# Small TensorE operations queued and issued one at a time between dense matmuls

## The chip, the cores and the metric

The kernel runs on one core of a Trainium2 chip. A core has a matrix engine (TensorE, PE in the profile; its weight loads are listed as PEld), a vector engine (VectorE, DVE), a scalar engine (ScalarE, ACT), GpSimd (POOL) and a queue engine for transfers (SyncE, SP). Each engine works through its own queue in order and waits for others through semaphores. TensorE writes to PSUM, eight banks that VectorE and ScalarE read. The metric is the device time of one execution in microseconds (us); several runs give a median. One further execution is recorded by the hardware profiler; its numbers are those of the profile.

## What is computed

Two layers act on x, 512 tokens by 2048 channels in float32. Both normalize, project, mix along the tokens, gate, project back, and add to the residual; then each adds a gated projection of a second input.

```python
for i in range(DEPTH):
    xn = rms_norm(h, norm_pre[i])
    if i % 2 == 0:
        proj = xn @ ab_w_in[j]                       # 2048 x 8336
        oa = forgetting_attention(...)               # 16 heads of 64, causal softmax
        ob = rwkv7_time_mix(...)                     # 16 heads of 64, a recurrence over tokens
        y = concat([oa * silu(ga), ob * silu(gb)]) @ ab_w_out[j]
    else:
        u, v, g = split(xn @ c_w_in[j])              # 2048 x 6144
        oc = chunked_spatial_gating(u, v, ...)
        y = (oc * silu(g)) @ c_w_out[j]
    h = h + rms_norm(y, norm_post[i])
    h = h + (p[i] @ ple_w_proj[i]) * sigmoid(h @ ple_w_gate[i])
```

## The kernel before

**Dense products.** Every dense operand is split into a high and a low part in a reduced float32 form, and a product is three matmuls: high by high, high by low, low by high. In the first layer `dense_fm` (L205 on) computes 128 output channels for all 512 tokens: it goes through 16 k-tiles of 128 channels, three matmuls each (L213, L214, L215), 512 columns wide. The weights come through `stream`: one transfer into a raw buffer, a cast on ScalarE (`whi`, L197) and a subtraction on VectorE (`wlo`, L199), each buffer holding four k-tiles, four buffers each. From the output product of the first layer on, the large products run in `seven`, which forms seven products of half matrices in place of eight (L1601). Some of these have the weights as the stationary side and 256 moving columns (`fm=True`: the two output products and the first gate), the others 512 moving columns.

**Side work.** While dense products run, everything else is woven in by hand. `weave` takes a list of (beat, step); after each k-tile `beat` counts up and runs the steps that are due. In `seven`, `later` and `tick` do the same. So the order of TensorE's queue is the order written, except where the scheduler of the framework finds that an operation's inputs would not be there in time by its own estimate; it then issues a later one that is ready.

The side steps that the change touches put several small TensorE operations into the queue at once:

- `rwkv_head` (matmuls at L484): for a pair of heads and half of the tokens, four chunks e, and for each the two heads q. The operands of head 0 lie in partitions 0 to 63, those of head 1 in 64 to 127, so each product uses half the rows of the array. The two accumulators are a `tm` tile and the `g` tile. Behind them stand masks on VectorE (L488 on) and copies on ScalarE. There are 16 such calls: eight pairs, two halves. The places are HEAD and HEAD1, in units of a window of 36 beats.
- `rwkv_tokens`: four transposes of the scaled keys (L515) into one `tm` tile, and two of the values (L523) into the next, then copies. 16 calls.
- `rwkv_chain`: the recurrence over eight chunks, three steps a chunk. The third step has the state update (L627) and the two products of the output, L636 and L637, in a row.
- `fox_load`'s `tokens` (L847): four transposes, 8 calls. `fox_probs` (L910): one to four transposes of attention weights, 64 calls, 160 transposes. `fox_values` (L923) multiplies by them.
- `flip` in `last_layer` (L1316): four transposes, 16 calls. `turn` in `layer_c` (L1760): four transposes, 16 calls, of which eight are placed in the second layer's output product.

Products of plain float32 operands (L484, L612 to L637, and the 32x32 ones of `rwkv_inverse` at L551 and L572) are run as two passes of the array; a transpose is one pass. `tm()` gives the names `tm0` and `tm1` in turn; each is one PSUM bank, so a third tile waits for the first. A single transpose of a mixing weight (L1716) and one of 16 rows (L1799) stand alone in `layer_c`; the change leaves them as they are.

Of the kernel before, what the change touches and what calls it, by code (L numbers as in the profile page):

```python
# [16 lines left out]
P = 128  # L17
# [89 lines left out]
class Net:  # L107
# [19 lines left out]
    def tm(self):  # L127
        self.ntm ^= 1
        return f"tm{self.ntm}"
# [76 lines left out]
    def dense_fm(self, wap, c0, xhi, xlo, ps, kts=None):  # L206


        nc = self.nc
        nk = len(xhi)  # L210
        acc = self.t(ps, [P, T], "mm")
        for k, hi, lo in self.stream(wap, c0, P, kts or list(range(nk)), None):
            nc.tensor.matmul(acc, hi, xhi[k], start=(k == 0), stop=False)  # L213
            nc.tensor.matmul(acc, hi, xlo[k], start=False, stop=False)  # L214
            nc.tensor.matmul(acc, lo, xhi[k], start=False, stop=(k == nk - 1))  # L215
            self.beat()
        return acc

    def weave(self, side, late=False):


        rest = [(n - self.beats, step) for n, step in self.side]
        if not late:
            for _, step in rest:
                step()
            rest = []
        self.side, self.beats = sorted([*rest, *side], key=lambda x: x[0]), 0

    def beat(self):
        self.beats += 1  # L230
        while self.side and self.side[0][0] <= self.beats:
# [238 lines left out]
    def rwkv_head(self, st, h, wp, ps):  # L470
# [11 lines left out]
        for e in range(GC):  # L482
# [4 lines left out]
        for n, pp in enumerate(BLOCKS):  # L487
            nc.vector.tensor_tensor(  # L488
                AT[pp], pg[n // 2][pp, :, 0, BLOCKS[n % 2]], self.mB[pp].broadcast_to([32, GC, 32]), ALU.mult
            )  # L490
        nc.vector.tensor_tensor(off, AT, bc(self.lev[1], P, 32), ALU.mult)
        nc.vector.tensor_tensor(off, off, bc(self.idst, P, 32), ALU.add)
        nc.vector.transpose(flip, off)
        for q in range(2):
            nc.scalar.copy(A32[BLOCKS[2 * q]], pg[q][BLOCKS[2 * q], :, 0, 32:64])
# [8 lines left out]
    def rwkv_tokens(self, st, h, wp, ps):  # L504
# [8 lines left out]
        pb = self.t(ps, [P, GC, P], self.tm())  # L513
        for e in range(GC):
            nc.tensor.transpose(pb[:, e, :], BKh[:, e, :], self.ident)  # L515
        BKt = self.t(wp, [P, GC, P], "BKt")
        nc.scalar.copy(BKt, pb)
# [3 lines left out]
        pv = self.t(ps, [P, GC // 2, P], self.tm())  # L521
        for m in range(GC // 2):
            nc.tensor.transpose(pv[:, m, :], v[:, o + m * P : o + m * P + P], self.ident)  # L523
        sv = SV.rearrange("p (m a) q i -> p m a q i", a=2)
        for a, src in enumerate((slice(0, 64), slice(64, 128))):
            nc.scalar.copy(sv[0:64, :, a, 1, :], pv[src, :, 64:128])
            nc.scalar.copy(sv[64:128, :, a, 0, :], pv[src, :, 0:64])
        nc.gpsimd.tensor_copy(UV[0:64, :, 1, :], SV[0:64, :, 1, :])
        nc.gpsimd.tensor_copy(UV[64:128, :, 0, :], SV[64:128, :, 0, :])
        st["hf", h] = dict(SV=SV, UV=UV, BKt=BKt)  # L530
        yield
# [70 lines left out]
    def rwkv_chain(self, st, h, wp, ps):  # L602
# [5 lines left out]
        for e in range(GC):  # L608
# [27 lines left out]
            nc.tensor.matmul(py[:, 0:P], fl(SV), fl(AR[:, e, 2:4, :]), start=True, stop=False)  # L636
            nc.tensor.matmul(py[:, 0:P], uv, st["GR", h][:, e, :], start=False, stop=True)  # L637
            nc.scalar.copy(Yt[0:64, cc * 64 : cc * 64 + 64], py[0:64, 0:64])
            nc.scalar.copy(Yt[64:128, cc * 64 : cc * 64 + 64], py[64:128, 64:128])
            yield  # L640

    def rwkv_fin(self, pr, st, wp, ps):
        nc, c, Yt = self.nc, self.cols, st["Yt"]
        col = lambda n: c[n][:, pr : pr + 1]
        yp = self.parts(Yt, wp, "bs")
# [24 lines left out]
    def rwkv_all(self, dense, first, wp, ps):  # L670
# [62 lines left out]
        def begin(pr):  # L733
            S0 = sts[pr]["hf", 0]["SV"][:, 0]
# [84 lines left out]
    def fox_load(self, pr, cols, dense, wp, ps):  # L819
# [24 lines left out]
        def tokens():  # L844
            pv = self.t(ps, [P, 4, P], self.tm())
            for m in range(4):
                nc.tensor.transpose(pv[:, m, :], vT[:, m * P : (m + 1) * P], self.ident)  # L847
            for q in range(2):
                v4 = V[q].rearrange("p (m t) -> p m t", t=P)
                src = pv[:, :, q * 64 : q * 64 + 64]  # L850
                nc.scalar.copy(v4[:, :, 0:64], src)
# [1251 lines left out]
```

## Time and profile before

| | us |
|---|---|
| median of 3 runs | 2201.89 |
| lowest, highest | 2201.17, 2202.13 |
| the profiled execution | 2202.32 |
| its span, first to last instruction | 2200.6 |
| mean granted TensorE clock | 0.998 |

The first layer's dense products run to about 740 us with the recurrence beside them, and to about 1012 us with the attention; `seven` begins there. The page gives, for each engine, its busy time; matmuls overlap, so the busy time of TensorE counts some stretches twice over in effect, and distances between starts say more than durations. In the timeline, rows of the same line that follow each other at once are merged, with their count behind an x.

### The profile page before, as it was taken

Reading aid. Unit: us, or ns where it says so; the run is one execution under the profiler, and the core shown is the slowest. Engines: PE = TensorE matmul, PEld = TensorE weight load, DVE = VectorE, ACT = ScalarE, POOL = GpSimd, SP = SyncE. Lnnn points to the kernel's source line nnn. Section 1 sums busy time; section 2 is a strip of 40 time slices with the busy share of each in tenths; the row PEclk is TensorE's granted clock in tenths of the full one; section 3 lists DMA queues with packets and bytes.
Section 4 is the critical chain, followed back from the end, with each engine's and each line's share of the span. In section 5 each row is a group of like instructions: output and inputs, shape, how many; then the busy total and the mean of one; then the engine's idle time right before and its main releaser. Section 6 shows DMA issues by size and latency. Waiting matters only on the chain.

```text
span 2200.6 us, 43486 instructions
## 1 busy us (share of the span) xinstructions
PE 2176.7 (99%) x16535; PEld 1870.7 (85%) x16535; DVE 1661.6 (76%) x3227; ACT 1354.0 (62%) x2763; POOL 298.4 (14%) x360
## 2 busy tenths in 40 slices
PE   8999999999999999999999999999999999999998
PEld 7878888888888788889999999887888889999886
DVE  8756677657633687887979978987687688878968
ACT  5545555555543577776767757755576577667754
POOL 2001010101000000000120121111221220120121
PEclk9999999999999999999999999999999999999999
DMA  7322322223233733336688889789779887688696
GB/s 240 94 80 58 90 78 71 71 73 85 69 85 101 214 106 91 106 92 182 151 200 273 215 187 237 177 219 229 171 163 231 184 201 190 146 199 274 191 253 163
DMA packets 304288, 343.35 MB, mean 156 GB/s; under 512 B 15773, under 2 KB 188222, under 8 KB 303054
## 3 DMA queue, kind: packets, MB, share of 16 engines
q1 hardware_dynamic: 237582, 240.93, 35.1%
q0 software_dynamic: 44608, 85.99, 22.7%
q10 hardware_dynamic: 21888, 13.64, 2.2%
q8 instruction: 130, 2.13, 0.4%
q14 instruction: 80, 0.66, 0.1%
HBM read 305.61 MB, written 34.90 MB: 155 GB/s over the span
## 4 chain that ended last, share of the span: by engine, by line
PE 89%; DMA 4%; DVE 3%; ACT 2%; issue 1%; SPq 0%; ACTq 0%; DVEq 0%; POOLq 0%
PE mm L1601 46%; PE mm L213 10%; PE mm L215 9%; PE mm L214 9%; DMA rq<-in_ple_w_gate_dram 2%; PE tm L551 1%; PE tm L572 1%; DMA gz<-gd 1%; PE g L923 1%; DVE wlo L1566 1%; PE pp L340 1%; PE tm L484 1%; PE ch L636 1%; PE tm L910 1%; PE ch L637 1%
## 5 line engine op out<-in xcount | busy, mean ns | idle before, releaser
L1564 ACT CAST whi<-rq 128x512 fp32r<-128x512 f32 x485 | 298.7, 621 | 203.4 <-PE mm L1601 126.1
L213 PE MATMUL mm<-xh,whi 128*128 128x512 f32 x992 | 412.0, 415 | 0.0
L1566 DVE TENSOR_TENSOR wlo<-rq,whi 128x512 fp32r<-128x512 f32 x485 | 331.0, 688 | 99.4 <-ACT whi L1564 96.8
L215 PE MATMUL mm<-xh,wlo 128*128 128x512 f32 x992 | 391.9, 395 | 0.0
L214 PE MATMUL mm<-xl,whi 128*128 128x512 f32 x992 | 390.0, 393 | 0.0
L197 ACT CAST whi<-raw 128x512 fp32r<-128x512 f32 x272 | 167.5, 617 | 148.5 <-PE mm L214 102.5
L199 DVE TENSOR_TENSOR wlo<-raw,whi 128x512 fp32r<-128x512 f32 x272 | 185.7, 695 | 91.7 <-ACT whi L197 68.9
L215 PEld LDWEIGHTS mm<-xh,wlo 128*128 128x128 f32 x992 | 186.4, 188 | 41.1
L213 PEld LDWEIGHTS mm<-xh,whi 128*128 128x128 f32 x992 | 187.1, 189 | 33.4
L214 PEld LDWEIGHTS mm<-xl,whi 128*128 128x128 f32 x992 | 187.3, 189 | 29.8
L1601 PE MATMUL mm<-whi,yh 128*128 128x512 f32 x424 | 137.0, 391 | 0.9 <-ACT whi L1564 0.9
L1601 PE MATMUL mm<-whi,xl 128*128 128x512 f32 x424 | 137.7, 392 | 0.0
L1601 PE MATMUL mm<-whi,yl 128*128 128x512 f32 x420 | 137.6, 393 | 0.0
L1566 DVE TENSOR_TENSOR wlo<-raw,whi 128x512 fp32r<-128x512 f32 x154 | 105.1, 688 | 36.0 <-ACT whi L1564 35.5
L1564 ACT CAST whi<-raw 128x512 fp32r<-128x512 f32 x154 | 94.7, 620 | 60.8 <-PE mm L1601 46.6
L1601 PE MATMUL mm<-xh,whi 128*128 128x256 f32 x696 | 126.9, 283 | 0.0
L1601 PEld LDWEIGHTS mm<-xh,whi 128*128 128x128 f32 x696 | 108.7, 192 | 0.1
L1509 POOL DMA_DIRECT2D rq<-in_c_w_in_dram x56 | 68.5, 1231 | 243.6 <-DVE wlo L1566 164.0
L1566 DVE TENSOR_TENSOR half<-rq,half 128x512 fp32r<-128x512 f32 x111 | 76.3, 688 | 32.6 <-ACT half L1564 32.4
L1601 PE MATMUL mm<-xh,wlo 128*128 128x256 f32 x348 | 98.5, 283 | 0.0
L1564 ACT CAST half<-rq 128x512 fp32r<-128x512 f32 x111 | 68.9, 620 | 47.6 <-PE mm L1601 27.6
L1601 PE MATMUL mm<-xl,whi 128*128 128x256 f32 x520 | 95.5, 284 | 0.1
(534 smaller groups left out, 5156.1 us busy)
## 6 DMA issues: line engine op xcount, KB each, us to landing
raw<-in_ab_w_in_dram SPq DMA_DIRECT2D x128, 512.0 KB, 3.9
rq<-in_c_w_in_dram POOLq DMA_DIRECT2D x56, 512.0 KB, 7.0
rq<-in_c_w_in_dram SPq DMA_DIRECT2D x50, 512.0 KB, 6.1
rq<-in_ple_w_gate_dram SPq DMA_DIRECT2D x44, 512.0 KB, 6.6
rq<-in_ple_w_gate_dram POOLq DMA_DIRECT2D x36, 512.0 KB, 9.1
raw<-in_c_w_in_dram SPq DMA_DIRECT2D x26, 512.0 KB, 7.9
rq<-in_c_w_out_dram SPq DMA_DIRECT2D x24, 512.0 KB, 4.5
rq<-in_ab_w_out_dram POOLq DMA_DIRECT2D x20, 512.0 KB, 6.9
```

Source lines behind the costliest of these rows:

```text
L197: nc.scalar.copy(hi[:, : m * n], src)
L199: self.weng.tensor_tensor(lo[:, : m * n], src, f(hi[:, : m * n]), ALU.subtract)
L213: nc.tensor.matmul(acc, hi, xhi[k], start=(k == 0), stop=False)
L214: nc.tensor.matmul(acc, hi, xlo[k], start=False, stop=False)
L215: nc.tensor.matmul(acc, lo, xhi[k], start=False, stop=(k == nk - 1))
L340: nc.tensor.matmul(acc, mat, part, start=(j == 0), stop=(j == 1))
L484: nc.tensor.matmul(pg[q][:, e], BK[pp, e].rearrange("p a t -> p (a t)"), AR[pp, e, q::2, :], start=True, stop=True)
L551: nc.tensor.matmul(px[dst, e, :], a[src, e, :], b[src, e, :], start=True, stop=True)
L1509: nc.gpsimd.dma_start(view(tl), block(*where), accum_op=ALU.add)
L1564: self.cast = nc.scalar.copy(hi, src)
L1566: nc.vector.tensor_tensor(lo, src, f(hi), ALU.subtract)
L1601: nc.tensor.matmul(o, x, y, start=(first and r == 0 and j == 0 and not a), stop=(r == 7 and j == 2), **more)
```

## The change

A queue `pe` is added. `spread` puts a step's TensorE operations into it, with what has to follow the last of them (`end`). The first goes out at once if the queue is empty. Each further one goes out from `between`, which is called after the first and the second matmul of each k-tile in `dense_fm`, after the third where no side step is due, and after every matmul in `seven`; it is tied behind the matmul before it with `issue_after`, which orders the two on their engine and adds no wait on another. `drain` empties the queue: before a new `tm` tile while operations on PSUM tiles of that kind are pending, at every `weave`, before `rwkv_fin`, the start of a pair, `fox_values`, and the last output product. In the products with 256 moving columns (`packed`) the queue is emptied at once, so that a step's operations stand in a row there as before.

In `rwkv_head` one operation of the queue is both products of a chunk e, so four operations. In `rwkv_tokens` it is one transpose, six in all; both `tm` tiles are now taken first. In `rwkv_chain` the two output products are two operations, and where a state update stands before them the queue starts with an empty place, so that a dense matmul comes between. In `fox_load`, `fox_probs`, `flip` and `turn` it is one transpose; these four are changed alike, and `fox_probs` stands for them below. No arithmetic is added or taken away, and no transfer is changed.

```diff
@@ -125,6 +125,8 @@
         return pool.tile(shape, dt, tag=tag, name=self.nm(tag), bufs=bufs)
     def tm(self):
+        if any(banks for *_, banks in self.pe):
+            self.drain()
         self.ntm ^= 1
         return f"tm{self.ntm}"
...
@@ -210,24 +212,52 @@
         nk = len(xhi)
         acc = self.t(ps, [P, T], "mm")
         for k, hi, lo in self.stream(wap, c0, P, kts or list(range(nk)), None):
-            nc.tensor.matmul(acc, hi, xhi[k], start=(k == 0), stop=False)
-            nc.tensor.matmul(acc, hi, xlo[k], start=False, stop=False)
-            nc.tensor.matmul(acc, lo, xhi[k], start=False, stop=(k == nk - 1))
+            self.between(nc.tensor.matmul(acc, hi, xhi[k], start=(k == 0), stop=False))
+            self.between(nc.tensor.matmul(acc, hi, xlo[k], start=False, stop=False))
+            self.mm = nc.tensor.matmul(acc, lo, xhi[k], start=False, stop=(k == nk - 1))
             self.beat()
         return acc
+    def spread(self, ops, end, banks=True):
+
+        now = not self.pe
+        self.pe.extend([*((op, None, banks) for op in ops[:-1]), (ops[-1], end, banks)])
+        if now:
+            self.between()
+        if self.packed:
+            self.drain()
+
+    def between(self, mm=None):
+        if mm is not None:
+            self.mm = mm
+        if self.pe:
+            op, end, _ = self.pe.popleft()
+            if op is not None:
+                with self.tc.issue_after(self.mm.ins) if self.mm is not None and not self.packed else nullcontext():
+                    op()
+            if end is not None:
+                end()
+
+    def drain(self):
+        while self.pe:
+            self.between()
+
     def weave(self, side, late=False):
+        self.drain()
         rest = [(n - self.beats, step) for n, step in self.side]
         if not late:
             for _, step in rest:
                 step()
+                self.drain()
             rest = []
         self.side, self.beats = sorted([*rest, *side], key=lambda x: x[0]), 0
     def beat(self):
         self.beats += 1
+        if not self.side or self.side[0][0] > self.beats:
+            self.between()
         while self.side and self.side[0][0] <= self.beats:
             self.side.pop(0)[1]()
...
@@ -479,20 +509,24 @@
         GR = st["GR", h] = self.t(wp, [P, GC, P], "GR")
         pg = [self.t(ps, [P, GC, 2, 64], tag) for tag in (self.tm(), "g")]
-        for e in range(GC):
+        def both(e):
             for q, pp in enumerate(halves):
                 nc.tensor.matmul(
                     pg[q][:, e], BK[pp, e].rearrange("p a t -> p (a t)"), AR[pp, e, q::2, :], start=True, stop=True
                 )
-        for n, pp in enumerate(BLOCKS):
-            nc.vector.tensor_tensor(
-                AT[pp], pg[n // 2][pp, :, 0, BLOCKS[n % 2]], self.mB[pp].broadcast_to([32, GC, 32]), ALU.mult
-            )
-        nc.vector.tensor_tensor(off, AT, bc(self.lev[1], P, 32), ALU.mult)
-        nc.vector.tensor_tensor(off, off, bc(self.idst, P, 32), ALU.add)
-        nc.vector.transpose(flip, off)
-        for q in range(2):
-            nc.scalar.copy(A32[BLOCKS[2 * q]], pg[q][BLOCKS[2 * q], :, 0, 32:64])
+
+        def masks():
+            for n, pp in enumerate(BLOCKS):
+                nc.vector.tensor_tensor(
+                    AT[pp], pg[n // 2][pp, :, 0, BLOCKS[n % 2]], self.mB[pp].broadcast_to([32, GC, 32]), ALU.mult
+                )
+            nc.vector.tensor_tensor(off, AT, bc(self.lev[1], P, 32), ALU.mult)
+            nc.vector.tensor_tensor(off, off, bc(self.idst, P, 32), ALU.add)
+            nc.vector.transpose(flip, off)
+            for q in range(2):
+                nc.scalar.copy(A32[BLOCKS[2 * q]], pg[q][BLOCKS[2 * q], :, 0, 32:64])
+
+        self.spread([lambda e=e: both(e) for e in range(GC)], masks)
         yield
         for q, po in enumerate(reversed(halves)):
             nc.vector.tensor_tensor(
...
@@ -510,24 +544,31 @@
         nc.gpsimd.tensor_tensor(
             BKh, BK.rearrange("p c a t -> p c (a t)"), PC.broadcast_to([P, GC, P]), ALU.mult
         )
-        pb = self.t(ps, [P, GC, P], self.tm())
-        for e in range(GC):
-            nc.tensor.transpose(pb[:, e, :], BKh[:, e, :], self.ident)
+        pb, pv = (self.t(ps, [P, n, P], self.tm()) for n in (GC, GC // 2))
         BKt = self.t(wp, [P, GC, P], "BKt")
-        nc.scalar.copy(BKt, pb)
         UV = self.t(wp, [P, GC, 2, 64], "UV")
         SV = self.t(wp, [P, GC, 2, 64], "SV")
         o = h * GC * 64
-        pv = self.t(ps, [P, GC // 2, P], self.tm())
-        for m in range(GC // 2):
+
+        def keys(e):
+            nc.tensor.transpose(pb[:, e, :], BKh[:, e, :], self.ident)
+
+        def values(m):
             nc.tensor.transpose(pv[:, m, :], v[:, o + m * P : o + m * P + P], self.ident)
-        sv = SV.rearrange("p (m a) q i -> p m a q i", a=2)
-        for a, src in enumerate((slice(0, 64), slice(64, 128))):
-            nc.scalar.copy(sv[0:64, :, a, 1, :], pv[src, :, 64:128])
-            nc.scalar.copy(sv[64:128, :, a, 0, :], pv[src, :, 0:64])
-        nc.gpsimd.tensor_copy(UV[0:64, :, 1, :], SV[0:64, :, 1, :])
-        nc.gpsimd.tensor_copy(UV[64:128, :, 0, :], SV[64:128, :, 0, :])
+
+        def end():
+            nc.scalar.copy(BKt, pb)
+            sv = SV.rearrange("p (m a) q i -> p m a q i", a=2)
+            for a, src in enumerate((slice(0, 64), slice(64, 128))):
+                nc.scalar.copy(sv[0:64, :, a, 1, :], pv[src, :, 64:128])
+                nc.scalar.copy(sv[64:128, :, a, 0, :], pv[src, :, 0:64])
+            nc.gpsimd.tensor_copy(UV[0:64, :, 1, :], SV[0:64, :, 1, :])
+            nc.gpsimd.tensor_copy(UV[64:128, :, 0, :], SV[64:128, :, 0, :])
+
         st["hf", h] = dict(SV=SV, UV=UV, BKt=BKt)
+        self.spread([
+            *(lambda e=e: keys(e) for e in range(GC)), *(lambda m=m: values(m) for m in range(GC // 2)),
+        ], end)
         yield
     def rwkv_inverse(self, st, wp, ps):
...
@@ -633,15 +674,24 @@
                             pS[pp, q * 64 : q * 64 + 64], ALU.mult, ALU.add,
                         )
             py = self.t(ps, [P, T], "ch")
-            nc.tensor.matmul(py[:, 0:P], fl(SV), fl(AR[:, e, 2:4, :]), start=True, stop=False)
-            nc.tensor.matmul(py[:, 0:P], uv, st["GR", h][:, e, :], start=False, stop=True)
-            nc.scalar.copy(Yt[0:64, cc * 64 : cc * 64 + 64], py[0:64, 0:64])
-            nc.scalar.copy(Yt[64:128, cc * 64 : cc * 64 + 64], py[64:128, 64:128])
+
+            def state(py=py, e=e, SV=SV):
+                nc.tensor.matmul(py[:, 0:P], fl(SV), fl(AR[:, e, 2:4, :]), start=True, stop=False)
+
+            def inner(py=py, e=e, uv=uv):
+                nc.tensor.matmul(py[:, 0:P], uv, st["GR", h][:, e, :], start=False, stop=True)
+
+            def out(py=py, cc=cc):
+                nc.scalar.copy(Yt[0:64, cc * 64 : cc * 64 + 64], py[0:64, 0:64])
+                nc.scalar.copy(Yt[64:128, cc * 64 : cc * 64 + 64], py[64:128, 64:128])
+
+            self.spread(([None] if cc < 7 else []) + [state, inner], out, False)
             yield
     def rwkv_fin(self, pr, st, wp, ps):
         nc, c, Yt = self.nc, self.cols, st["Yt"]
         col = lambda n: c[n][:, pr : pr + 1]
+        self.drain()
         yp = self.parts(Yt, wp, "bs")
         yield
         pm = self.blocksum(self.centr, yp, ps)
...
@@ -906,17 +962,23 @@
         nc = self.nc
         s, W = st["s", b], (b + 1) * P
         pt = self.t(ps, [P, T], self.tm())
-        for m in range(b + 1):
+
+        def one(m):
             nc.tensor.transpose(pt[:, m * P : (m + 1) * P], s[:, m * P : (m + 1) * P], self.ident)
-        p4 = pt[:, :W].rearrange("p (m t) -> p m t", t=P)
-        hi, lo = (x[:, 0 : b + 1, b, :] for x in st["PT"])
-        with self.tc.high_priority(SPRI):
-            nc.scalar.copy(hi, p4)
-            nc.vector.tensor_tensor(lo, p4, f(hi), ALU.subtract)
+
+        def end():
+            p4 = pt[:, :W].rearrange("p (m t) -> p m t", t=P)
+            hi, lo = (x[:, 0 : b + 1, b, :] for x in st["PT"])
+            with self.tc.high_priority(SPRI):
+                nc.scalar.copy(hi, p4)
+                nc.vector.tensor_tensor(lo, p4, f(hi), ALU.subtract)
+
+        self.spread([lambda m=m: one(m) for m in range(b + 1)], end)
     def fox_values(self, q, st, head, y, ps):
         nc = self.nc
         own, oth = (slice(x * 64, x * 64 + 64) for x in (q, 1 - q))
+        self.drain()
         po = self.t(ps, [P, T], "g")
         for m in range(4):
             for j in range(2):
...
@@ -1023,6 +1085,7 @@
             self.homes = {}
             self.turns = 0
             self.tied, self.entry = False, None
+            self.pe, self.packed, self.mm = deque(), False, None
             self.clock, self.todo = 0, []
             self.ahead = {}
             self.weng = tc.nc.vector
...
@@ -1572,6 +1641,8 @@
         nc, tc = self.nc, self.tc
+        self.drain()
+        self.packed = fm
         for step, (pr, prod, keep) in enumerate(order):
             first = prod not in (2, 3)
             if first:
...
@@ -1598,9 +1669,9 @@
                                     o, ms = acc[m], slice(m * P, (m + 1) * P)
                                     parts = (xh[:, ms], hi), (xh[:, ms], lo), (xl[:, ms], hi)
                                 for j, (x, y) in enumerate(parts):
-                                    nc.tensor.matmul(
+                                    self.between(nc.tensor.matmul(
                                         o, x, y, start=(first and r == 0 and j == 0 and not a), stop=(r == 7 and j == 2), **more
-                                    )
+                                    ))
                     rows = []
                 self.tick()
             for m in range(2):
```

More of the change, by code (lines that the diff above doesn't have):

```diff
@@ L845, in tokens @@
             pv = self.t(ps, [P, 4, P], self.tm())
-            for m in range(4):
+            def one(m):
                 nc.tensor.transpose(pv[:, m, :], vT[:, m * P : (m + 1) * P], self.ident)
[L848 to L851, printed above, removed]
-                nc.vector.tensor_tensor(v4[:, :, 64:128], src, f(v4[:, :, 0:64]), ALU.subtract)
+            def end():
+                for q in range(2):
+                    v4 = V[q].rearrange("p (m t) -> p m t", t=P)
+                    src = pv[:, :, q * 64 : q * 64 + 64]
+                    nc.scalar.copy(v4[:, :, 0:64], src)
+                    nc.vector.tensor_tensor(v4[:, :, 64:128], src, f(v4[:, :, 0:64]), ALU.subtract)
+            self.spread([lambda m=m: one(m) for m in range(4)], end)
         return (Q, KH, KL, V), tokens
@@ L908, in fox_probs, with one, end @@
         pt = self.t(ps, [P, T], self.tm())
-        for m in range(b + 1):
+        def one(m):
             nc.tensor.transpose(pt[:, m * P : (m + 1) * P], s[:, m * P : (m + 1) * P], self.ident)
-        p4 = pt[:, :W].rearrange("p (m t) -> p m t", t=P)
-        hi, lo = (x[:, 0 : b + 1, b, :] for x in st["PT"])
-        with self.tc.high_priority(SPRI):
-            nc.scalar.copy(hi, p4)
-            nc.vector.tensor_tensor(lo, p4, f(hi), ALU.subtract)
+        def end():
+            p4 = pt[:, :W].rearrange("p (m t) -> p m t", t=P)
[4 more added lines that the diff above has]
+        self.spread([lambda m=m: one(m) for m in range(b + 1)], end)
     def fox_values(self, q, st, head, y, ps):
@@ L1264, in x4 @@
             s[3] = self.place(("xh", 2))
+        self.drain()
         for q in range(4):
@@ L1313, in flip, with one, end @@
             pt = self.t(ps, [P, T], "mm")
-            for j in range(4):
+            def one(j):
                 src = H[2 * g + j // 2, m // 2][:, j % 2, m % 2 * P : m % 2 * P + P]
                 nc.tensor.transpose(pt[:, j * P : (j + 1) * P], src, self.ident)
-            if m < 2:
-                if m == 0 and g % 2 == 0:
-                    self.fl = self.t(self.xp, [P, 4, T], f"xh{1 - g // 2}")
-                o = self.fl[:, g % 2 * 2 + m, :]
-            else:
-                o = self.slot("yl", 2 * g + m - 2, F32)
-            res[g, m] = o
-            nc.scalar.copy(o, pt)
+            def end():
+                if m < 2:
+                    if m == 0 and g % 2 == 0:
+                        self.fl = self.t(self.xp, [P, 4, T], f"xh{1 - g // 2}")
+                    o = self.fl[:, g % 2 * 2 + m, :]
+                else:
+                    o = self.slot("yl", 2 * g + m - 2, F32)
+                res[g, m] = o
+                nc.scalar.copy(o, pt)
+            self.spread([lambda j=j: one(j) for j in range(4)], end)
         def late(q):
@@ L1574, in seven @@
         nc, tc = self.nc, self.tc
+        self.drain()
+        self.packed = fm
         for step, (pr, prod, keep) in enumerate(order):
@@ L1757, in turn, with one, end @@
             pt = self.t(ps, [P, 2, 256], "mm")
-            for a in range(2):
-                for m in range(2):
-                    nc.tensor.transpose(pt[:, a, m * P : (m + 1) * P], src(a, 2 * e + m), self.ident)
-            fs[q, e] = self.slot("yl" if q < 4 else "xl", 2 * (q % 4) + e, F32).rearrange("p (a t) -> p a t", a=2)
-            nc.scalar.copy(fs[q, e], pt)
+            def one(a, m):
+                nc.tensor.transpose(pt[:, a, m * P : (m + 1) * P], src(a, 2 * e + m), self.ident)
+            def end():
+                fs[q, e] = self.slot("yl" if q < 4 else "xl", 2 * (q % 4) + e, F32).rearrange("p (a t) -> p a t", a=2)
+                nc.scalar.copy(fs[q, e], pt)
+            self.spread([lambda a=a, m=m: one(a, m) for a in range(2) for m in range(2)], end)
         def early(q, at):
```

## The prediction

> **What bounds the kernel now.** I read the page's table of engines first, then its chain that ended last.
>
> ```profile
> span 2200.6 us, 43486 instructions
> PE 2176.7 (99%) x16535; PEld 1870.7 (85%) x16535; DVE 1661.6 (76%) x3227; ACT 1354.0 (62%) x2763; POOL 298.4 (14%) x360
> ...
> PE 89%; DMA 4%; DVE 3%; ACT 2%; issue 1%; SPq 0%; ACTq 0%; DVEq 0%; POOLq 0%
> PE mm L1601 46%; PE mm L213 10%; PE mm L215 9%; PE mm L214 9%; DMA rq<-in_ple_w_gate_dram 2%; PE tm L551 1%; PE tm L572 1%; DMA gz<-gd 1%; PE g L923 1%; DVE wlo L1566 1%; PE pp L340 1%; PE tm L484 1%; PE ch L636 1%; PE tm L910 1%; PE ch L637 1%
> ```
>
> TensorE is busy for 99% of the span and holds 89% of the chain. So the time is, nearly, the sum of what each matmul adds to TensorE's row of matmuls, and the change must be priced there. A busy time is no price, since matmuls overlap. I take the distance from start to start, and because the first matmul after a small one is recorded early and its successor late, I measure from the last dense matmul before a group to the **second** dense one behind it, and take off two plain dense steps. The next view is TensorE's timeline around one whole head (L484).
>
> ```profile
> 85.52 0.39 PE L213 MATMUL mm<-xh,whi 128*128 128x512 f32 x1
> 85.75 0.39 PE L214 MATMUL mm<-xl,whi 128*128 128x512 f32 x1
> 85.97 0.39 PE L215 MATMUL mm<-xh,wlo 128*128 128x512 f32 x1
> 86.29 0.37 PE L484 MATMUL tm<-AR,BK 64*128 64x128 f32 x1
> 86.30 0.37 PE L484 MATMUL g<-AR,BK 64*128 64x128 f32 x1
> 86.50 0.27 PE L484 MATMUL tm<-AR,BK 64*128 64x128 f32 x1
> ...
> 87.17 0.27 PE L484 MATMUL tm<-AR,BK 64*128 64x128 f32 x1
> 87.18 0.27 PE L484 MATMUL g<-AR,BK 64*128 64x128 f32 x1
> 87.38 0.50 PE L213 MATMUL mm<-xh,whi 128*128 128x512 f32 x1
> 87.72 0.39 PE L214 MATMUL mm<-xl,whi 128*128 128x512 f32 x1
> ```
>
> Columns are start, duration, engine and line. A plain dense step is 0.23 us (85.52 to 85.75). A head is four calls of two products, each product two passes: 16 passes, in 8 pairs that start together, one of a pair on the upper 64 rows of the array and one on the lower (86.29 and 86.30). From 86.50 to 87.17 there are six pair steps: 0.67/6 = 0.112 us each. The whole group costs 87.72 - 85.97 - 2 x 0.23 = 1.29 us. Eight pairs at 0.112 are 0.90; the other **0.39 to 0.40 us is paid once a group**. It is seen at both ends: the first pair starts 0.32 after the dense matmul in place of 0.23, the second 0.21 after the first in place of 0.11, and the next dense one 0.20 after the last pair, its successor 0.34 after it. A half-row product neither enters nor leaves under a dense matmul.
>
> **The change, part by part.**
>
> *Heads.* The four calls go to four places, with a dense matmul between. Each then pays the constant itself: 0.40 + 2 x 0.112 = 0.62 us, four of them 2.50, against 1.29 now: +1.20 us a head, that is three constants.
>
> ```profile
> L484 PE MATMUL tm<-AR,BK 64*128 64x128 f32 x128 | 19.2, 288 | 0.8 <-DVE BK L464 0.8
> L484 PE MATMUL g<-AR,BK 64*128 64x128 f32 x128 | 18.9, 289 | 0.1
> ...
> L910 PE MATMUL tm<-ident,s 128*128 128x128 f32 x160 | 28.1, 273 | 0.8 <-DVE s L901 0.8
> ...
> L636 PE MATMUL ch<-AR,SV 128*128 128x128 f32 x128 | 25.1, 278 | 0.0
> L637 PE MATMUL ch<-GR,UV 128*128 128x128 f32 x128 | 25.0, 277 | 0.0
> ```
>
> These are groups by line and form; 256 passes of L484 are 16 heads. Two of them, pair 1's, wait for their operands in a stretch where VectorE is late:
>
> ```profile
> PE tm L484 <- DVE BK L464: 0.8, 2, 0.6
> PE ch L627 <- DVE UV L622: 0.5, 1, 0.5
> ```
>
> ```profile
> 160.00:170.00 10.00, 8.85 (x44) 7.00 (x43) 9.63 (x29) 2.81 (x8) 0.74 (x1) 0.83 0.22 60
> ```
>
> The first two rows are TensorE's waits (total, times, longest), the third is the table of windows for the stretch 160 to 170: VectorE busy 9.63 of 10 us. Where the operands come after the four places have passed, the four calls are ready together and still run in a row. So I count 14 heads: 14 x 3 = 42 new groups x 0.40 = **+16.8 us**. No row shows a lone call of a head, so it is bounded by neighbours. The nearest lone partial-row operation is one transpose of 16 rows:
>
> ```profile
> 1402.22 0.39 PE L1601 MATMUL mm<-whi,yl 128*128 128x512 f32 x1
> 1402.54 0.23 PE L1799 MATMUL mm<-ident,sq 16*128 16x16 f32 x1
> 1402.70 0.50 PE L1601 MATMUL mm<-whi,yl 128*128 128x512 f32 x1
> 1403.04 0.40 PE L1601 MATMUL mm<-wlo,yl 128*128 128x512 f32 x1
> ```
>
> It costs 1403.04 - 1402.22 - 0.46 = 0.36, less one pass of 0.11: a constant of 0.25. That is the low end: 42 x 0.25 = 10.5. The high end is all 16 heads at 0.40: 48 x 0.40 = 19.2. I take 0.40, since it comes from this very operation and shape.
>
> *Full-row transposes and products.* The gain the change could have is here: a weight load that no longer follows another small one. The two cases stand in the trace side by side, a lone transpose (L1716, which the change leaves alone) and a row of four (L1316):
>
> ```profile
> 1601.88 0.39 PE L1601 MATMUL mm<-whi,xh 128*128 128x512 f32 x1
> 1602.11 0.27 PE L1716 MATMUL mm<-ident,accq 128*128 128x128 f32 x1
> 1602.13 0.47 PE L1601 MATMUL mm<-whi,xh 128*128 128x512 f32 x1
> 1602.45 0.39 PE L1601 MATMUL mm<-wlo,xh 128*128 128x512 f32 x1
> ...
> 2053.61 0.39 PE L1601 MATMUL mm<-whi,xh 128*128 128x512 f32 x1
> 2053.84 0.60 PE L1316 MATMUL mm<-ident,xh 128*128 128x128 f32 x4
> 2054.20 0.48 PE L1601 MATMUL mm<-whi,yl 128*128 128x512 f32 x1
> 2054.51 0.40 PE L1601 MATMUL mm<-wlo,yl 128*128 128x512 f32 x1
> ```
>
> Lone: 1602.45 - 1601.88 - 0.46 = 0.11 us. Four in a row: 2054.51 - 2053.61 - 0.46 = 0.44, so 0.11 each. The lone one looks cheap, its dense successor starting 0.02 later, but that successor's own successor comes 0.32 on. Standing alone saves nothing; to the rows' last digit it costs between 0 and 0.01 more. Lone two-pass products exist too:
>
> ```profile
> 137.90 0.40 PE L215 MATMUL mm<-xh,wlo 128*128 128x512 f32 x1
> 138.13 0.39 PE L612 MATMUL ch<-SV,AR 128*128 128x128 f32 x2
> 138.27 0.48 PE L213 MATMUL mm<-xh,whi 128*128 128x512 f32 x1
> 138.59 0.40 PE L214 MATMUL mm<-xl,whi 128*128 128x512 f32 x1
> ```
>
> 138.59 - 137.90 - 0.46 = 0.23, twice 0.115. How many new places there are is a count from the code: L910 has 160 transposes in 64 calls, so 96 more places; the two chain products leave the row of L627, 128; the token transposes of a head leave some 58 of at most 80, since the next head's tile empties the queue; L1316 has 48; L1760 has 24, because half its calls fall in a product whose moving side is 256 wide, where the queue is emptied at once; the attention's tokens have 6, since the value product empties the queue. That is about 360 places x 0.005 = **+1.8 us**, bounds 0 and 3.6.
>
> *What moves with them.* The work behind a group (masks, copies, casts) now follows its last operation: for a head 3 x 0.23 + 1.20 = 1.9 us later. VectorE runs in order, and behind the four masks stand the splits of the next weights (wlo), for which TensorE waits. Their own row says how much room there is:
>
> ```profile
> DVE wlo L199 <- ACT whi L197: 68.9, 59, 3.0
> ```
>
> VectorE arrives at these splits early, 68.9 us in total, and four buffers of four k-tiles each hold 11 us of dense work. The inverse that reads the masks is placed several beats behind the head. No DMA moves. I cost it at nothing; if the cover went, it would be up to 1.9 us for a head. Waits that vanish bound the other side: slower heads give VectorE time in the stretch above, where 0.8 + 0.5 us of waits and 10 x (1 - 0.83) = 1.7 us of lost clock (0.83 is the granted clock there) could go. So -3.0 to +3.0, value 0: VectorE's backlog in that stretch follows from dense results that come later too.
>
> **Sum.** 16.8 + 1.8 = 18.6 on the profiled execution of 2202.3 us (span 2200.6 and 1.7 around it): 2220.9. The median of the runs shown, 2201.9, is 0.4 below that execution, so I predict **2220.5 us**.
>
> **The rivals.**
>
> *A lone weight load is hidden (faster).* The mechanism: in dense, small, dense, the small one's load runs under the dense matmul before it, and the next dense load under the small one's stream, so a lone pass costs only its stream, 128/512 of a dense step: 0.23/4 = 0.06 in place of 0.11. It decides for this side if most operations gain that. Some 410 full-row operations would stand quite alone (the 360 and the first of each old row that is freed): -0.05 x 410 = -20.5. A head's constant would lose the exposed load of the dense matmul behind it, one step of 0.11: 42 x 0.29 = +12.2. On the profiled execution 2202.3 - 20.5 + 12.2 = 2194.0, as a median **2193.6**. Against it: L1716 stands alone and costs 0.11. The Trainium skill, "TensorE: Matmul & The Clock Gate", Part 2, says that the next tile's weights load while this tile's matmul runs, which read plainly gives this rival; the trace agrees for a load under a dense matmul and not under a 128-wide one. Chance 0.04.
>
> *The rows stay rows.* If the order on TensorE is set by readiness and not by the place written, all small operations may still be issued together, or the queue may be emptied nearly everywhere. Then 2202. For it: pair 1's heads already run late. Against: TensorE's list of waits names heads and transposes hardly at all (0.8 us each), so their inputs are there at the place written. Chance 0.05.
>
> *The clock drops in the heads.* A head's stretch, 2.5 us of half-used array and 0.7 of dense, might lose clock like the stretch at 160. One such window cost 1.7 us: 14 x 1.7 = 24 more, 2244. Against: there the array waited for operands; a lone call's gaps are under 0.3 us. The same page, Part 1, puts the re-throttling at idle gaps of some 3 us, and by that rule no head would lose clock; no run here has shown a spread head. Chance 0.04.
>
> **How the numbers follow.** Forecast, slower by about 0.85%: chance 0.87. Low end: 10.5 + 0 - 3.0 = +7.5, 2209; high end: 19.2 + 3.6 + 3.0 = +25.8, 2228, and 2 more for a pair step that may be longer alone. The range 2209 to 2230 leaves out the three rivals, 0.13. A change of 0.2%, 4.4 us, is about what a measurement of this kernel can tell from none. Faster 0.04, within 0.05, slower 0.91.
>
> **What would show it.** In the changed kernel's timeline: groups of four L484 passes with 0.32 ahead, and a second dense start 0.62 + 0.46 behind the first; L484 in 50 to 64 groups in place of 16; lone L910 and L1316 still at 0.11. TensorE's busy share stays at 99%. The growth must lie before 610 us, where the heads are, with almost none between 740 and 2200. I am wrong if lone heads cost clearly under 0.5 us, if lone transposes fall to 0.06, or if the growth lies in waits for VectorE.

## The result and the profile after

| | before | after |
|---|---|---|
| median, us | 2201.53 (4 runs) | 2224.32 (4 runs) |
| lowest, highest | 2200.40, 2202.13 | 2223.56, 2229.24 |
| ratio after/before, 95% interval | | 1.0109, 1.0091 to 1.0126 |

The change makes the kernel slower by 22.8 us; 18.6 were forecast. The profiled execution of the changed kernel is the longest of its four (2229.24, span 2227.5), so a second one, of the same kernel run again (e8, 2224.44), is read beside it wherever a few microseconds matter.

In the page of the kernel after, the table of engines and the chain that ended last:

```profile
span 2227.5 us, 43492 instructions
PE 2200.2 (99%) x16535; PEld 1870.5 (84%) x16535; DVE 1658.7 (74%) x3227; ACT 1357.3 (61%) x2763; POOL 303.5 (14%) x360
...
PE 85%; DVE 7%; ACT 4%; DMA 3%; issue 2%; SPq 0%; ACTq 0%; DVEq 0%; POOLq 0%
```

The same 16535 matmuls are spread over 26.9 us more, and TensorE is still busy for 99% of the span. So the time did not go into long waits: the matmuls themselves stand further apart. Where, two landmarks tell: four transposes of 16 rows stand where the first layer's recurrence ends, and `seven` begins with its first matmul of `yh` and `whi`. Before, in the view of one line's instructions (count, durations, first and last start):

```profile
L812 PE MATMUL tm<-ident,vT x4: 202/208/208, 747.3 to 747.5; 16*128 16x16 f32 x4
...
L1601 PE MATMUL mm<-yh,whi x424: 278/283/386, 1012.8 to 1973.4; 128*128 128x256 f32 x142
```

The same two lines after, under their new numbers:

```profile
L863 PE MATMUL tm<-ident,vT x4: 202/208/209, 767.4 to 767.6; 16*128 16x16 f32 x4
...
L1672 PE MATMUL mm<-yh,whi x424: 278/283/387, 1035.8 to 2001.1; 128*128 128x256 f32 x142
```

Up to the end of the recurrence the kernel loses 767.4 - 747.3 = 20.1 us, in the attention another 23.0 - 20.1 = 2.9, and over this matmul's range in `seven` 4.7 ((2001.1 - 1035.8) - (1973.4 - 1012.8)). The last does not repeat: the same range grows by 0.9 in e8, a second profile of the same kernel. The first two do.

A whole lead head after (L514 is L484 of before, L215 to L217 the dense product), in TensorE's timeline:

```profile
86.03 0.39 PE L217 MATMUL mm<-xh,wlo 128*128 128x512 f32 x1
86.35 0.37 PE L514 MATMUL tm<-AR,BK 64*128 64x128 f32 x1
86.36 0.37 PE L514 MATMUL g<-AR,BK 64*128 64x128 f32 x1
86.56 0.27 PE L514 MATMUL tm<-AR,BK 64*128 64x128 f32 x1
86.57 0.27 PE L514 MATMUL g<-AR,BK 64*128 64x128 f32 x1
86.77 0.50 PE L215 MATMUL mm<-xh,whi 128*128 128x512 f32 x1
87.20 0.37 PE L514 MATMUL tm<-AR,BK 64*128 64x128 f32 x1
...
89.33 0.50 PE L215 MATMUL mm<-xh,whi 128*128 128x512 f32 x1
89.66 0.39 PE L216 MATMUL mm<-xl,whi 128*128 128x512 f32 x1
```

A call begins 0.85 us after the one before (86.35 to 87.20): 0.23 for the dense matmul between them and 0.62 for the call. The head takes 89.66 - 86.03 - 5 x 0.23 = 2.48, against 1.29 in a row: 1.19 more. TensorE's timeline shows 16 groups of these products before and 59 after: 14 heads in four groups each, pair 1's first head in two and its second in one.

### The profile page after: what moved, and what is told of

Same layout as the page of the kernel before. It is cut to its first block, busy times and chain, and to the rows that moved or that the text cites. A ratio compares the mean times of both kernels' runs of the same rounds, so it can differ in the third digit from the quotient of the medians.

```text
span 2227.5 us, 43492 instructions
## 1 busy us (share of the span) xinstructions
PE 2200.2 (99%) x16535; PEld 1870.5 (84%) x16535; DVE 1658.7 (74%) x3227; ACT 1357.3 (61%) x2763; POOL 303.5 (14%) x360
## 4 chain that ended last, share of the span: by engine, by line
PE 85%; DVE 7%; ACT 4%; DMA 3%; issue 2%; SPq 0%; ACTq 0%; DVEq 0%; POOLq 0%
PE mm L1672 43%; PE mm L215 9%; PE mm L217 9%; PE mm L216 9%; PE tm L592 1%; DMA rq<-in_c_w_in_dram 1%; DVE wlo L1635 1%; PE tm L514 1%; PE tm L613 1%; PE g L985 1%; DMA rq<-in_ple_w_gate_dram 1%; ACT yh L882 1%; PE ch L679 1%; PE ch L682 1%; ACT whi L199 1%
## 5 line engine op out<-in xcount | busy, mean ns | idle before, releaser
L215 PE MATMUL mm<-xh,whi 128*128 128x512 f32 x992 | 415.6, 419 | 0.0
L217 PE MATMUL mm<-xh,wlo 128*128 128x512 f32 x992 | 402.4, 406 | 0.7 <-DVE wlo L201 0.7
L216 PE MATMUL mm<-xl,whi 128*128 128x512 f32 x992 | 403.0, 406 | 0.0
L201 DVE TENSOR_TENSOR wlo<-raw,whi 128x512 fp32r<-128x512 f32 x272 | 185.4, 693 | 88.9 <-ACT whi L199 66.6
L217 PEld LDWEIGHTS mm<-xh,wlo 128*128 128x128 f32 x992 | 186.5, 188 | 43.7 <-DVE wlo L201 2.0
L215 PEld LDWEIGHTS mm<-xh,whi 128*128 128x128 f32 x992 | 187.1, 189 | 34.6
L1672 PEld LDWEIGHTS mm<-whi,yh 128*128 128x128 f32 x424 | 79.6, 188 | 19.2 <-ACT whi L1633 2.2
```

Of the source, the lines that this page charges most:

```text
L201: self.weng.tensor_tensor(lo[:, : m * n], src, f(hi[:, : m * n]), ALU.subtract)
L215: self.between(nc.tensor.matmul(acc, hi, xhi[k], start=(k == 0), stop=False))
L216: self.between(nc.tensor.matmul(acc, hi, xlo[k], start=False, stop=False))
L217: self.mm = nc.tensor.matmul(acc, lo, xhi[k], start=False, stop=(k == nk - 1))
L1672: self.between(nc.tensor.matmul(o, x, y, start=(first and r == 0 and j == 0 and not a), stop=(r == 7 and j == 2), **more))
```

## The experiments

The theory was that a half-row product pays about 0.40 us each time it is entered from, and left for, a full-row dense matmul, so that cutting 14 groups into 56 is nearly all of the change. Its rivals were that standing alone costs something for any small operation, that the other spread steps (tokens, chain, attention, flips) carry a share, and that the masks and copies that come later make TensorE wait. The results together; "growth" is measured in each profile by the two landmarks, against before:

| run | head groups | growth to the recurrence's end | in the attention | median (runs) | ratio to before, 95% |
|---|---|---|---|---|---|
| after | 59 | 20.1 | 2.9 | 2224.32 (4) | 1.0109, 1.0091 to 1.0126 |
| e8 after, again | 59 | 18.3 | 2.8 | 2223.77 (4) | 1.0104, 1.0084 to 1.0124 |
| e2 heads alone spread | 58 | 18.6 | 1.0 | 2222.60 (4) | 1.0103, 1.0088 to 1.0119 |
| e5 heads in two groups | 31 | 9.9 | 2.7 | 2214.33 (4) | 1.0060, 1.0044 to 1.0077 |
| e1 heads in a row | 20 | 4.0 | 2.9 | 2209.20 (4) | 1.0044, 1.0027 to 1.0060 |
| e6 heads, tokens in rows | 20 | 1.8 | 2.8 | 2205.89 (9) | 1.0025, 1.0015 to 1.0034 |
| e7 and probabilities too | 20 | 1.6 | -0.9 | 2202.89 (10) | 1.0011, 1.0001 to 1.0020 |
| e3 128-row heads, spread | 58 | 10.8 | 2.9 | 2217.04 (4) | 1.0077, 1.0062 to 1.0092 |
| e4 128-row heads, in a row | 19 | 8.4 | 2.9 | 2215.37 (4) | 1.0069, 1.0054 to 1.0084 |

The kernel before measured 2199.65 beside e1 to e4 and 2200.78 (18 runs) beside e5 to e8.

**e1: the heads back in rows, all else as changed.**

```diff
-        self.spread([lambda e=e: both(e) for e in range(GC)], masks)
+        for e in range(GC):
+            both(e)
+        masks()
```

> The change as it is, but the four calls of each head stand in a row again; transposes and chain products stay spread. Theory A (each further group of half-row products pays about 0.40 us, lone full-row ones pay nearly nothing): the heads' loss goes, 43 groups fewer, 2224.3 - 17 = 2207, at least under 2209; what is left over before (3 to 6 us) is chain, attention and waits. Rival B (any operation standing alone costs, some 0.06 us each over 360 places): most of the loss stays, 2218 or more.

It takes back 13 to 14 of the 23 us, where 17 were expected. That the heads are the largest part stands; that they are all of it does not: 9.6 us stay. Part of it is seen in e1's timeline of a head, whose two halves have come apart (`g` takes one half of the rows, `tm` the other):

```profile
285.64 0.39 PE L216 MATMUL mm<-xl,whi 128*128 128x512 f32 x1
285.96 1.16 PE L514 MATMUL g<-AR,BK 64*128 64x128 f32 x8
287.04 0.51 PE L217 MATMUL mm<-xh,wlo 128*128 128x512 f32 x1
...
290.13 0.40 PE L216 MATMUL mm<-xl,whi 128*128 128x512 f32 x1
290.52 1.16 PE L514 MATMUL tm<-AR,BK 64*128 64x128 f32 x8
291.61 0.50 PE L217 MATMUL mm<-xh,wlo 128*128 128x512 f32 x1
```

The eight passes into `g` go alone, and 4.6 us later the eight into `tm`. Without a partner on the other 64 rows eight passes take as long as eight pairs, and the constant is paid twice: 8 x 0.112 + 0.40 = 1.30 more. Three lead heads (at 286, 436 and 585 us) are split so; aligned matmul by matmul with before, each of those three stretches grows by 1.3 to 1.4 us, and the rest up to the recurrence's end by nothing on balance (1.6 us less around pair 1's heads, about as much more elsewhere). The likely reason is in the change to `rwkv_tokens`: it takes both `tm` tiles before its first transpose, so the head that follows finds none free, and the framework issues the half that needs none. e6 tests it.

**e2: the heads alone spread.** Every other `spread` is replaced by a call that issues the operations at once and then their `end`.

```diff
+    def inrow(self, ops, end, banks=True):
+        for op in ops:
+            if op is not None:
+                op()
+        end()
...
-        self.spread([
+        self.inrow([
```

> The kernel before with only the heads spread, everything else in rows. Theory A: 42 or 43 new groups x 0.40 = +17, 2218 to 2220. Rival B: four places a head x 16 x 0.06 = +4, 2206.

Up to the recurrence's end 18.6, as much as the change itself (18.3 and 20.1). All 14 heads are clean groups of four here. Aligned with before, there are seven stretches with two such heads: four grow by 2.4 us, three by 2.9 to 3.0, and between them little changes. So a head costs 1.2, as priced. What the three have more is one wait each, behind the first of their heads. Before, and in e2's timeline:

```profile
222.32 0.48 PE L215 MATMUL mm<-xh,wlo 128*128 128x512 f32 x1
```

```profile
226.99 0.50 PE L217 MATMUL mm<-xh,wlo 128*128 128x512 f32 x1 [0.24 <-DVE wlo L201]
```

This dense matmul now finds its low weights (`wlo`) not yet written by VectorE. From here on the kernel lies another 0.5 us behind; the same at two more places, 1.5 us together. The wait stands three times in after, e8, e2 and e3, whose heads are spread singly, and in none of the others. The agreement of 18.6 with the change is partly chance: e2's profile loses 0.6 us ahead of its first head, and gains nothing around pair 1's heads, where the change gains 1.2. The median, 2222.60, is above the 2218 to 2220 expected; in the profile the rest of it lies behind `seven`'s start, where this kernel's steps are written in rows as before.

**e3 and e4: is it the half rows, or the standing alone?** Both let each head product take all 128 rows, with masks of zeros, so that the recurrence's triangular parts are left out of what they compute; e3 keeps the products spread, e4 puts them in a row as in e1.

```diff
-                    pg[q][:, e], BK[pp, e].rearrange("p a t -> p (a t)"), AR[pp, e, q::2, :], start=True, stop=True
+                    pg[q][:, e], BK[:, e].rearrange("p a t -> p (a t)"), AR[:, e, q::2, :], start=True, stop=True
...
-            nc.vector.memset(tl, 1.0)
+            nc.vector.memset(tl, 0.0)
```

> The change, but each head product runs over all 128 rows in place of 64, and the masks behind the heads are all zero, so the recurrence's triangular parts are left out; the number of passes is unchanged, but they no longer run in pairs. Theory A (the constant belongs to leaving and entering the full-row form): a lone call costs 4 x 0.112 = 0.45 us in place of 0.62, so 64 calls give 64 x 0.17 = 11 us less than the change: 2213 or so, and within 2 us of the same kernel with the heads in rows. Rival C (the constant belongs to standing alone, whatever the rows): 64 x (0.40 + 0.45), 2239.

> As the one before (full-row head products, zero masks), with the four calls of each head in a row and the rest spread. Theory A: 16 passes x 0.112 = 1.79 us a head against 1.29 in half rows, so 8 us more than the kernel with only the heads put back: some 2214, equal to the spread full-row kernel within 2 us. Rival C: 17 us or more below the spread full-row kernel.

Spread or in a row now differs by 1.7 us, with intervals that overlap; with half rows it was 13 (23.0 in e8 less 9.6 in e1, each against its own before). In e3's timeline:

```profile
86.03 0.39 PE L217 MATMUL mm<-xh,wlo 128*128 128x512 f32 x1
86.25 0.38 PE L514 MATMUL tm<-AR,BK 128*128 128x128 f32 x2
86.47 0.39 PE L514 MATMUL g<-AR,BK 128*128 128x128 f32 x2
86.61 0.48 PE L215 MATMUL mm<-xh,whi 128*128 128x512 f32 x1
86.93 0.38 PE L514 MATMUL tm<-AR,BK 128*128 128x128 f32 x2
...
87.61 0.38 PE L514 MATMUL tm<-AR,BK 128*128 128x128 f32 x2
```

A lone call of four full-row passes begins 0.22 behind its dense matmul, not 0.32, and repeats every 0.68 (86.93 to 87.61): 0.23 for the dense matmul and 0.45 = 4 x 0.112. It has no constant, and is cheaper alone than the half-row call (0.62), though it runs no two passes side by side. That is 0.17 a call, 9.5 us for the 56 calls of 14 heads; up to the recurrence's end e3 is 7.5 below e8, and its waits for other operands are longer (1.9 us for `UV` in place of 0.5, and 0.4 for `GR`). In a row the half-row form wins: 1.29 a head against 16 x 0.112 = 1.79. Sixteen heads at 0.50 more are 8.0, and e4 grows by 8.4.

**e5: half as many groups.** Two calls of a head form one operation.

```diff
-        self.spread([lambda e=e: both(e) for e in range(GC)], masks)
+        self.spread([lambda e=e: (both(e), both(e + 1)) for e in range(0, GC, 2)], masks)
```

> The change with the four calls of a head queued as two operations of two calls each: half the new groups. Theory A (0.40 us a group): 27 groups fewer than the change's 59, 11 us faster than it, so 11 to 13 us above the kernel before. Rival B (each new place costs, whatever stands in it): 32 of some 400 places fewer, within 3 us of the change.

The first head, in e5's timeline:

```profile
86.05 0.39 PE L217 MATMUL mm<-xh,wlo 128*128 128x512 f32 x1
86.37 0.37 PE L514 MATMUL tm<-AR,BK 64*128 64x128 f32 x1
...
87.01 0.51 PE L215 MATMUL mm<-xh,whi 128*128 128x512 f32 x1
87.45 0.37 PE L514 MATMUL tm<-AR,BK 64*128 64x128 f32 x1
...
88.43 0.39 PE L217 MATMUL mm<-xh,wlo 128*128 128x512 f32 x1
```

88.43 - 86.05 - 3 x 0.23 = 1.69: one group more than in a row, 0.40 more. The growth falls with the groups: 28 fewer than in e8 and 8.4 less to the recurrence's end, 0.30 a group; in the medians 9.4 less, 0.34. That is under the 0.40 of a clean group, although e8 also has the three waits for late weights, 1.5 us, and e5 has none. Half groups bring a loss of their own: the second lead head, for one, comes earlier behind the first, and starts with two unpaired passes into `tm` before the first into `g` (at the same place in e3, TensorE's `g` pass waits 0.44 us for VectorE's mask `GR`). How much these losses come to was not measured singly.

**e6: heads and tokens in rows.** As e1, and `rwkv_tokens` as before, its second `tm` tile taken after the first four transposes.

```diff
-        pb, pv = (self.t(ps, [P, n, P], self.tm()) for n in (GC, GC // 2))
+        pb = self.t(ps, [P, GC, P], self.tm())
...
+        nc.scalar.copy(BKt, pb)
+        pv = self.t(ps, [P, GC // 2, P], self.tm())
```

> Heads in rows as in the first experiment, and the token transposes of a head in rows too, their second tile taken after the first four as in the kernel before; chain, attention and flips stay spread. Theory D (with both tiles taken at once, a following head finds its tm tile taken, so its two row halves run in separate groups, some 1.3 us for each of three heads, and 1 of its own): the recurrence falls by 4 us against the first experiment and every head is one group of 16 passes; the attention keeps its 3 us: 3 us above the kernel before, in the first layer. Rival E (the 4 us come from the chain's lone products): no change against the first experiment there.

The growth to the recurrence's end falls from 4.0 to 1.8. The three heads are split less, not whole: two passes into `g` go first, the other 14 stand together. So the tokens' two tiles explain most of the splitting and not all of it. The attention's 2.8 is untouched, and the median is 5.1 above before, where 3 was expected.

**e7: the attention's probabilities in rows too.** What still stands singly are the chain's output products, the attention's tokens, the flips and turns.

```diff
-        self.spread([lambda m=m: one(m) for m in range(b + 1)], end)
+        for m in range(b + 1):
+            one(m)
+        end()
```

> As the one before, with the transposes of the attention weights in rows too; spread are left the chain's two products, the attention's token transposes, and those of the second layer. Theory F (the attention's 3 us are the value products' waits for the copies behind the last transposes, which come later): attention within 0.5 us of the kernel before, the whole within 1.5 us of it. Rival B (lone operations cost): the chain's 128 places alone 0.06 each, 7 us.

The two landmarks of e7:

```profile
L859 PE MATMUL tm<-ident,vT x4: 201/208/208, 748.9 to 749.1; 16*128 16x16 f32 x4
...
L1670 PE MATMUL mm<-yh,whi x424: 278/283/386, 1013.5 to 1973.3; 128*128 128x256 f32 x142
```

The attention's growth is gone (1013.5 - 748.9 is 264.6, before 265.5), and `seven` starts within 0.7 us of before. The median is 2.1 us above before, where at most 1.5 was expected, its interval from 0.01% to 0.20%: with some 200 lone operations (128 + 48 + 24 + 6 by the prediction's counts) that is 0.01 us each, far from the 0.06 of the rival.

**e8: the change once more**, to see what in the first profile is the change's and what that execution's.

> The change itself once more beside these, for a second profile. Theory: the first layer 23 us longer than before, as in the first profile; the 4 us of waits in the second layer's first product, which came with late weights, need not return: 23 us above the kernel before in the median.

The median, 2223.77, repeats within 0.6 us, and the two growths within 1.8 and 0.1. The extra of the first profile in the second layer does not repeat. No version found here beats before; the best, e7, equals it within 0.2%.

## Why the prediction held, and where it was mis-sized

**What bounds the kernel: right.** The page of after still has TensorE at 99%, and the time follows the distances between starts.

**Heads, +16.8: right in mechanism, count and price.** The timeline after shows 0.62 for a lone call and 1.19 for a head against the 1.20 forecast. The count was 43 new groups against 42 forecast. In e2 the heads' stretches grow by 18.5, of which 1.5 are the late weights. That the constant belongs to the half-row form, and not to being alone, is shown by e3 and e4; that it is paid per group, by e5, and by e1's split heads. The Trainium skill, "TensorEngine Tiling (Array Packing)", section Key Properties, says that changing the tiling mode drains TensorE. The 0.40 agrees with that, the gap of 0.32 ahead of a half-row call and 0.22 ahead of a full-row one above all; the page gives no price, and no run here shows the drain itself.

**Pair 1's heads stay together: nearly.** Their first head fell into a group of eight `tm` and one of eight `g` passes, their second stayed whole. The stretch around them ran 1.2 us shorter than before. In the table of windows after, for 160 to 170 us, behind the busy times of the five engines stands the granted clock, 1.00, where it was 0.83 before:

```profile
160.00:170.00 10.00, 9.25 (x53) 7.36 (x52) 9.50 (x29) 3.40 (x9) 0.00 (x0) 1.00 0.19 52
```

The prediction had this gain among its bounds, and put it down to slower heads that give VectorE time. That reason falls: e1, with its heads in rows, has the same clock of 1.00 there and 1.6 us less than before. e2, with slow heads, has 0.91 there and 0.92 in the next 10 us, which is the same loss as before's 0.83 and 1.00, and no gain. Nor does TensorE wait less: from 150 to 180 us it is idle for 1.5 us before and for 1.5 after. What brings the gain was not tried alone; of the runs here only e2 has the chain's output products in a row. It may not be the change at all: the mean clock of before is 0.998 in the profile shown, and 0.999, as in the profiles of the change, in 14 of its 25 runs beside the experiments.

**Full-row operations, +1.8: right within what can be told.** A lone transpose in layer two, in the timeline after:

```profile
2081.34 0.39 PE L1672 MATMUL mm<-whi,xh 128*128 128x512 f32 x1
2081.58 0.27 PE L1381 MATMUL mm<-ident,xh 128*128 128x128 f32 x1
2081.60 0.48 PE L1672 MATMUL mm<-whi,yl 128*128 128x512 f32 x1
2081.92 0.27 PE L1381 MATMUL mm<-ident,xh 128*128 128x128 f32 x1
2081.95 0.48 PE L1672 MATMUL mm<-wlo,yl 128*128 128x512 f32 x1
2082.26 0.27 PE L1381 MATMUL mm<-ident,xh 128*128 128x128 f32 x1
```

One transpose and one dense matmul take 0.34 (81.58 to 81.92, 81.92 to 82.26), so 0.11 for the transpose, alone as in a row. The rival of a hidden load would have shown 0.29. It falls, and so does the rival of rows that stay rows, by the 59 groups.

**What moves with them, at nothing: this step failed.** The prediction looked at the work behind a group on VectorE, and asked whether it would be late for the next weights. It was, in three places: the waits (`PE mm L217 <- DVE wlo L201`) came to 0.7 us of idle time and, from start to start, to 1.5 us. That is inside the bounds given, and not nothing: the 68.9 us by which VectorE arrived early in total did not cover each single place. What the prediction did not price is what a longer hold on a tile, and a later end, do to TensorE's own order. TensorE's waits after, from 80 to 700 us:

```profile
PE tm L613 <- ACT BKt L560: 1.2, 5, 0.3
...
PE mm L217 <- DVE wlo L201: 0.7, 3, 0.2
```

The first of these rows is new. The copy `BKt` once followed the fourth token transpose and now follows the sixth, and the inverse that needs its `tm` tile (L613) waits 1.2 us in all. The row stands in every run with spread tokens and in none with tokens in a row. To it come the split heads: in the changed kernel six heads of the 14 begin with two `g` passes alone. With heads in rows this is worth 2.2 us (e1 to e6). With heads spread, compare the stretch behind pair 1, from 195 to 650 us of before: it grows by 15.8 in e2, where only the heads are spread, and by 17.4 and 18.9 in the two profiles of the change. So spread tokens and chain products cost 1.6 to 3.2 there; up to the recurrence's end this is hidden by the gain at pair 1 and by e2's own loss ahead of the heads.

The larger miss is the attention, which was to have almost no growth and has 2.9. (Its work adds 3.8 or so: of before's waits, that of the first L910 for `s`, 0.8 us, does not come in the changed kernel, and the kernel gains 1.0 there.) A tile of attention weights is now transposed over several beats, and the value product (L985, L923 of before) comes at its old place. Before, in the timeline:

```profile
809.39 0.39 PE L215 MATMUL mm<-xh,wlo 128*128 128x512 f32 x1
809.62 1.42 PE L923 MATMUL g<-PT,yh 128*128 128x512 f32 x8
...
811.59 0.39 PE L214 MATMUL mm<-xl,whi 128*128 128x512 f32 x1
```

The same place after:

```profile
829.71 0.40 PE L217 MATMUL mm<-xh,wlo 128*128 128x512 f32 x1
829.95 0.40 PE L985 MATMUL g<-PT,yh 128*128 128x512 f32 x1
830.18 0.27 PE L967 MATMUL tm<-ident,s 128*128 128x128 f32 x1
830.21 0.42 PE L943 MATMUL pp<-yh,yh 128*128 128x384 f32 x1
830.47 0.34 PE L944 MATMUL pp<-yh,yh 128*128 128x384 f32 x1
830.91 1.25 PE L985 MATMUL g<-PT,yh 128*128 128x512 f32 x7
...
832.29 0.40 PE L216 MATMUL mm<-xl,whi 128*128 128x512 f32 x1
```

The eight matmuls of the product are broken after the first, later work is put in, and the same instructions take 2.58 us (829.71 to 832.29) in place of 2.20 (809.39 to 811.59). Six of the 16 value products are broken so. TensorE's waits from 745 to 1035 us point to the cause, copies of the transposed weights that are not there yet:

```profile
PE g L985 <- DVE PT L974: 0.5, 1, 0.5
...
PE g L985 <- ACT PT L973: 0.2, 1, 0.2
```

e7 has neither of these two rows, no broken product, and no growth there. That the late copies, 0.7 us of waits in all, are the whole cause is not shown step by step; that spreading `fox_probs` costs the attention 3.7, e6 against e7 shows (2.8 and -0.9).

**The clock in the heads: falls.** The mean granted clock is 0.999 over the span in both profiles of the change; the lone calls' gaps cost no clock.

**The sum.** By the first layer's growth in e8: heads, late weights, tokens and chain, less the gain at pair 1, 18.3, attention 2.8, and some 2 of the 23.0 left for the second layer. The forecast had the heads right. That its 18.6 comes so near the 18.3 is partly luck, since late weights, tokens and chain, which it put nearly at nothing, are balanced in part by the gain at pair 1. It lacked the attention's 3.

Over `seven`'s range the kernels differ from before by -1.3 to 4.7 us, e2 with its unchanged order among the highest. Of e2's 4.7, a loss of clock near 1530 us, absent in before, accounts for some 1.6 (granted clock 0.91 from 1520 to 1540 us); the rest stays open.

## What to carry to other kernels

Before an operation is set apart from its like, ask in which form it enters the array: here full-row passes of TensorE stood between dense matmuls at the price of the row (0.11 a pass), while half-row pairs paid 0.40 a group to enter and to leave, and belong in one group. Spreading also lengthens the time from the first to the last operation of a step, so look who needs the tile that it holds, and who needs its result at a place that has not moved. A cover that is ample in total can still be missing at single places: look at it place by place. And TensorE, busy for 99% of the span, hid none of this: price the distance from start to start, at the second dense matmul behind.

## What the runs showed of the hardware

Half-row products are a bargain only in company: eight passes without a partner take as long as eight pairs (1.16 us recorded for eight in e1), and a lone call of four half-row passes in two pairs (0.62) takes longer than the same call as four full-row passes (0.45). And the same amount of waiting can lose clock or not: TensorE is idle for 1.5 us from 150 to 180 us before and after, at most 0.6 at a time, and the granted clock from 160 to 170 us was 0.83 in the profile before and 1.00 in the one after. What decides it is not shown.
